# Retention in two rows, sample parts side by side, paced queues: one change to a hybrid encoder step

## The chip, the core and the metric

The kernel runs on one core of one Trainium2 chip. The metric is the device time of one execution in microseconds (us); the time before is 1988.08 us, the median of three runs (1986.14 to 1988.54). The core has TensorE (PE; weight loads are listed as PEld), VectorE (DVE), ScalarE (ACT), GpSimd (POOL) and SyncE (SP), from whose queue all transfers of this kernel are issued. The engines run side by side and wait for each other by semaphores.

## The reference

One layer of a streaming encoder. A prompt of 2048 rows and a sample of 64 rows pass the same weights:

```python
h = rmsnorm(x, norm_g) @ w_in            # 1024 -> 6144 columns
qa, ka, va, za, qb, kb, vb, zb, ga, gb = split(h)
# A: differential attention, 4 heads, two 64-d halves, values 128-d, ALiBi, mask by chunks of 64
p = softmax(qa_c @ ka_c.T / 8 - slope * |i - j|)        # c = 0, 1
oa = (p[0] - lam * p[1]) @ va                            # the sample also sees 4096 cached frames
# B: retention, 4 heads of 128, decay g per head
ob = ((qb @ kb.T) * g**|i-j|) @ vb + (qb * g**(t+1)) @ state
state = g**n * state + kb.T @ (vb * g**(n-1-t))
m = sigmoid(ga) * ((rmsnorm(oa) * silu(za)) @ w_o_diff) + sigmoid(gb) * ((rmsnorm(ob) * silu(zb)) @ w_o_ret)
y = x + m @ w_out
```

Outputs are y for prompt and sample, the normalised keys, the values and the retention states of both.

## The kernel before

Every large product is taken in three matmuls. An operand is split into a rounded high part and the remainder (`xh`/`xl`, `wh`/`wl`), and hi times hi, hi times lo and lo times hi are added up in one PSUM bank.

*Streams.* `w_stream` runs the projections: weights come in pieces (`ws`), ScalarE rounds them (L462), GpSimd takes the remainder (L472), and `mm_group` (L500) multiplies. Columns for values, keys and queries of the attention and values of the retention are computed with tokens on the partitions (`natural`): 128 tokens at a time, and in the first half of the prompt the 64 sample tokens as a last, ninth tile. The others come transposed (`transposed`). A projection's result leaves its `mm` bank through `fin_va`, `fin_qk`, `fin_vb` or `fin_t`, whose copies on ScalarE are L770 and L772 (the latter with a scale), and goes to scratch in DRAM. `z_stream` runs the attention head by head (`qk_block`, scores at L956 and L957, masked on VectorE at L965; `softmax`, exponentials at L995; `at_pv`), after the first half the sample's attention (`sample_attn`, `sample_pv`), and the retention blocks of 128 rows (`ret_block`). When both are through, `out_stream` makes the output: `m_tile` (L1630 to L1632) and `y_tile` (L1698 to L1700), closed by `y_fin` (L1712).

*Order.* The order of PE, ACT and DVE instructions is written by a planner inside the kernel. Each stream is a generator; `loop` takes the first task by priority whose wake time has come. `P`, `A`, `V` and `G` advance a clock per engine by an assumed duration; `take` and `give` hand buffers on with the time at which they come free. PE work of lower priority, mostly projections, so fills the places where a stream has to wait. The order on POOL and SP follows from the order in which instructions are handed out.

*Buffers.* Ten rows of 128 x 1024 (`ROWS`) serve scores, retention and the sample. PSUM has two banks each for `mm`, `s` (scores) and `at` (transposes of the attention, output tiles) and one each for `pv` and `tp`.

*Retention block.* `ret_block` takes two rows (`rqk`, `rvx`) for queries, keys and values, and, when its turn in the chain of states comes, a third (`rru`) for the output. The output is squared (L1434), summed (L1440), normalised (`rsqrt_small`, L229 to L235, then L1446), transposed through `tp` (L1452), copied (L1455) and stored. `ret_some` keeps two blocks alive and returns when the last is done.

*Sample attention.* A head's 64 queries times two halves fill 128 partitions. Its eight units of 512 keys are exponentiated one after the other (L1186). `sample_pv` then sums, moves two sums, the tail and the four halves of the other partitions over by transfers, weighs the two softmax halves (L1274, L1277) and multiplies with the values (L1294). At the end `fold` (L1194) adds the two halves by a matmul.

Of the kernel before, what the change touches and what calls it, by code (L numbers as in the profile page):

```python
# [36 lines left out]
LAT = 250.0  # L37
DMA_LAT = 2600.0
# [22 lines left out]
class Hybrid:  # L61
# [78 lines left out]
    st = ld  # L140
# [26 lines left out]
    def consts(self):  # L167
# [7 lines left out]
        self.fold = c("fold", [128, 64])  # L175
# [47 lines left out]
    def rsqrt_small(self, ms, n, ready):  # L223
# [12 lines left out]
        for _ in range(3):  # L236
            self.tr = self.V(20, self.act)
# [86 lines left out]
    def norm_log(self, j):  # L324
        nc = self.nc
        ss, ms, y, t = self.xin[j][9:]
        nc.scalar.activation(y, ss, AF.Ln, scale=1.0 / D, bias=self.epst[:y.shape[0]])
        nc.scalar.activation(y, y, AF.Exp, scale=-0.5)
        self.A(1, 0, 40)
        self.xin[j].append(self.A(1, 0, 40))  # L330

    def norm_mean(self, j):
        ss, ms, y, t = self.xin[j][9:13]
        self.nc.vector.tensor_scalar(ms, ss, 1.0 / D, EPS, op0=ALU.mult, op1=ALU.add)
        self.V(1, t)

    def norm_root(self, j):
# [6 lines left out]
        for _ in range(3):  # L344
            self.V(20, t2)
# [23 lines left out]
    def x_tile(self, j, wait=True, mid=None):  # L369
# [6 lines left out]
        for q in range(2):  # L376
# [14 lines left out]
            self.give(tag, t2)  # L391
            if q == 0 and mid:
# [98 lines left out]
    def mm_group(self, ps, n, us, wsl, x, wfirst, last, between=None):  # L491
        nc = self.nc
        seg, xsl = x
        for c in range(KC):
# [3 lines left out]
            ops = ((a, xh), (a, xl), (b, xh)) if wfirst else ((xh, a), (xh, b), (xl, a))  # L498
            for i, (p, q) in enumerate(ops):
# [10 lines left out]
    def opening(self, fin):  # L510
# [5 lines left out]
        self.x_alloc(1)  # L516
        us, low = [], []
# [46 lines left out]
        for j in range(1, 9):  # L564
# [15 lines left out]
            ps = self.psum("mm")  # L580
# [3 lines left out]
            self.spawn(fin(ps[:r], r, 1, 128 * j if j < 8 else T, self.pe + LAT), 0, "w")  # L584
            yield self.pe

    def natural(self, half, fin, fresh=False, wide=False):
# [6 lines left out]
        for j0 in range(0, len(tiles), per):  # L594
# [3 lines left out]
            for u, (src, r, seg, col) in enumerate(group):  # L598
                if fresh:
                    yield lambda: len(self.xt_ready) > j0 + u  # L600
                    yield self.xt_ready[j0 + u]
                yield from self.mm_group(ps[:r, n * u:n * u + n], n, us, slice(0, n),
# [4 lines left out]
            self.spawn(fin(ps[:r, :n * len(group)], r, len(group), t0, self.pe + LAT), 0, "w")  # L607
            yield self.pe

# [6 lines left out]
    def fin_qk(self, which, g, nh=2):  # L616
# [4 lines left out]
        def fin(ps, r, nu, t0, t):  # L621
# [16 lines left out]
            self.give("mm", max(t1, t2))  # L638
# [10 lines left out]
            t = self.V(8)  # L649
# [3 lines left out]
            t = self.V(n)  # L653
# [42 lines left out]
    def fin_va(self, g, nh=2):  # L696
# [4 lines left out]
        def fin(ps, r, nu, t0, t):  # L701
# [13 lines left out]
            self.give("mm", max(t2, t3))  # L715
# [17 lines left out]
    def fin_vb(self, g):  # L733
# [3 lines left out]
        def fin(ps, r, nu, t0, t):  # L737
# [5 lines left out]
            self.give("mm", t)  # L743
# [50 lines left out]
    def rms_t(self, ps, n, gain, t, tag, tmp=None):  # L794
# [35 lines left out]
        self.A(n, t)  # L830
# [14 lines left out]
        else:  # L845
            yield t
            nc.vector.scalar_tensor_tensor(out=o, in0=o, scalar=gain, in1=y, op0=ALU.mult, op1=ALU.mult)
            t = self.V(n, t)
# [134 lines left out]
    def softmax(self, st, nk, b, pair):  # L983
# [4 lines left out]
        for units, mx, t in st:  # L988
# [11 lines left out]
        for c in range(2):  # L1000
            lsum = ls[c][:, 0:1]
            if len(rows[0]) > 1:
                lsum = sp.tile([128, 1], F32, tag="a_ls", name="a_ls")
                nc.vector.tensor_add(lsum, ls[c][:, 0:1], ls[c][:, 1:2])
                self.V(1, t)
            nc.vector.reciprocal(w[:, c:c + 1], lsum)
            self.V(1, t)
        nc.vector.tensor_mul(w[:, 1:2], w[:, 1:2], self.nlam)
        t = self.V(1, t)
        yield t  # L1010
        for k, (u0, u1) in enumerate(zip(rows[0], rows[1])):
            n = u0.shape[1]
            nc.scalar.activation(u1, u1, AF.Identity, scale=w[:, 1:2])  # L1013
            t1 = self.A(n, t, 90)
# [3 lines left out]
            t2 = self.V(n, t1)  # L1018
# [73 lines left out]
    def sample_attn(self):  # L1092
# [9 lines left out]
        for h in range(4):  # L1102
# [42 lines left out]
            for m in range(9):  # L1145
# [12 lines left out]
                if m < 8:  # L1158
# [3 lines left out]
                    t = self.V(512, t)  # L1162
# [19 lines left out]
            self.A(64, t, 220)  # L1182
            te = []
            for m in range(8):
                u = units[m // 2][:, (m % 2) * 512:(m % 2) * 512 + 512]
                nc.scalar.activation(u, u, AF.Exp, bias=mx[:, m:m + 1], scale=-1.0, accum_out=lp[:, m:m + 1])  # L1186
                te.append(self.A(512, t, 220))
            self.spawn(self.sample_pv(h, units, both, tail, te, lp, oall), 2, "z")
# [4 lines left out]
        for h in range(4):  # L1193
            nc.tensor.matmul(fp[:, 64 * h:64 * h + 64], oall[:, 128 * h:128 * h + 128], self.fold,  # L1194
# [29 lines left out]
    def v_split(self):  # L1224

        nc = self.nc
        for m in 4 * [*range(9)]:
# [11 lines left out]
            t = self.V(128 * nt, t)  # L1239
# [3 lines left out]
    def sample_pv(self, h, units, both, tail, te, lp, oall):  # L1243
# [7 lines left out]
        l, num, den = (sp.tile([128, 1], F32, tag=k, name=k, bufs=3) for k in ("s_l", "s_num", "s_den"))  # L1251
        nc.vector.tensor_reduce(l, lp[:, :9], axis=AX.X, op=ALU.add)
        nc.vector.tensor_copy(num[lo], l[lo])
        nc.vector.tensor_copy(den[up], l[up])
# [3 lines left out]
        self.ld(num[up], l[lo], 1 << 12)  # L1258
        t = self.ld(den[lo], l[up], 1 << 12)
        tt = sp.tile([64, 64], F32, tag="s_tt", name="s_tt", bufs=2)  # L1260
# [4 lines left out]
        yield t + 600  # L1265
        nc.vector.reciprocal(den, den)
# [665 lines left out]
```

## Time and profile before

| | us |
|---|---|
| median of three runs | 1988.08 |
| profiled execution, its own time | 1990.07 |
| its span | 1988.3 |
| TensorE busy | 1963.8 |
| VectorE busy | 1057.2 |
| ScalarE busy | 991.0 |
| GpSimd busy | 417.3 |

The profile page comes from one execution. A group's row names line, engine, operation, output<-input, shapes and count, then busy time, mean length of one in ns, and the idle time of the engine before it with what ended it. A matmul's printed length runs to the end of its result and overlaps the next one, so the pace is read from start to start. A row of the timeline has the start, the length, engine, line and operation, `rows*columns` of the stationary operand, and in brackets the idle time before it. A row of the list of waits has total, number and longest. `L` numbers are lines of the kernel before; in the changed kernel they are larger.

### The profile page before, as it was taken

Reading aid. Unit: us, or ns where it says so; the run is one execution under the profiler, and the core shown is the slowest. Engines: PE = TensorE matmul, PEld = TensorE weight load, DVE = VectorE, ACT = ScalarE, POOL = GpSimd, SP = SyncE. Lnnn points to the kernel's source line nnn. Section 1 sums busy time; section 2 is a strip of 40 time slices with the busy share of each in tenths; the row PEclk is TensorE's granted clock in tenths of the full one; section 3 lists DMA queues with packets and bytes.
Section 4 is the critical chain, followed back from the end, with each engine's and each line's share of the span. In section 5 each row is a group of like instructions: output and inputs, shape, how many; then the busy total and the mean of one; then the engine's idle time right before and its main releaser. Section 6 shows DMA issues by size and latency. Waiting matters only on the chain.

```text
span 1988.3 us, 34106 instructions
## 1 busy us (share of the span) xinstructions
PE 1963.8 (99%) x12206; PEld 1754.7 (88%) x12206; DVE 1057.2 (53%) x2786; ACT 991.0 (50%) x2185; POOL 417.3 (21%) x383
## 2 busy tenths in 40 slices
PE   9999999999999999999999999999999999999999
PEld 7778989998998989999998888888888888889997
DVE  6453665446565326547756656525644356444432
ACT  6432666655454436436757656635744544333330
POOL 2310121212121221221111111211122434222210
PEclk9999999999999999999999999999999999999999
DMA  7646553335665756664352342652233666444431
GB/s 245 200 143 177 138 157 118 117 87 152 174 174 152 174 151 196 200 187 137 102 153 81 109 137 62 175 146 85 70 98 114 202 219 206 141 130 148 131 93 53
DMA packets 332508, 285.21 MB, mean 143 GB/s; under 512 B 65905, under 2 KB 297329, under 8 KB 332338
## 3 DMA queue, kind: packets, MB, share of 16 engines
q1 hardware_dynamic: 332338, 283.03, 48.5%
q8 instruction: 96, 1.57, 0.3%
q14 instruction: 74, 0.61, 0.1%
HBM read 187.19 MB, written 91.49 MB: 140 GB/s over the span
## 4 chain that ended last, share of the span: by engine, by line
PE 64%; DVE 2%; DMA 2%; ACT 1%; issue 0%; POOL 0%; SPq 0%; POOLq 0%; ACTq 0%; DVEq 0%
PE mm L500 31%; PE at L1698 3%; PE at L1699 3%; PE at L1700 3%; PE s L956 2%; PE s L957 2%; PE at L1063 2%; PE mm L1630 2%; PE s L1632 2%; PE mm L1631 2%; PE mm L1632 2%; PE s L1631 2%; PE s L1630 2%; PE pv L1043 1%; PE pv L1042 1%; PE pv L1041 1%
## 5 line engine op out<-in xcount | busy, mean ns | idle before, releaser
L500 PE MATMUL mm<-xh,wh 128*128 128x512 f32 (+2 forms) x1280 | 459.3, 359 | 2.8 <-ACT ev L770 2.8
L500 PE MATMUL mm<-xh,wl 128*128 128x512 f32 (+2 forms) x1280 | 452.4, 353 | 0.0
L500 PE MATMUL mm<-xl,wh 128*128 128x512 f32 (+2 forms) x1280 | 451.8, 353 | 0.0
L472 POOL TENSOR_TENSOR wl<-ws,wh 128x512 fp32r<-128x512 f32 x189 | 258.6, 1381 | 867.2 <-ACT wh L462 605.5
L500 PE MATMUL mm<-wh,xh 128*128 128x256 f32 (+3 forms) x864 | 273.5, 317 | 0.3 <-DVE tlo L713 0.3
L500 PEld LDWEIGHTS mm<-xh,wh 128*128 128x128 f32 x1280 | 241.4, 189 | 32.4 <-ACT ev L770 3.3
L500 PEld LDWEIGHTS mm<-xh,wl 128*128 128x128 f32 x1280 | 241.1, 188 | 31.9 <-POOL wl L472 0.4
L500 PE MATMUL mm<-wh,xl 128*128 128x256 f32 (+3 forms) x864 | 267.9, 310 | 0.1
L500 PE MATMUL mm<-wl,xh 128*128 128x256 f32 (+3 forms) x864 | 267.6, 310 | 0.0
L500 PEld LDWEIGHTS mm<-xl,wh 128*128 128x128 f32 x1280 | 241.6, 189 | 27.8
L1078 DVE TENSOR_TENSOR atl<-at,ath 128x512 fp32r<-128x512 f32 (+1 forms) x144 | 93.9, 660 | 159.2 <-ACT ath L1076 159.2
L500 PEld LDWEIGHTS mm<-wh,xh 128*128 128x128 f32 (+1 forms) x864 | 162.8, 188 | 11.8 <-PE s L957 0.4
L500 PEld LDWEIGHTS mm<-wl,xh 128*128 128x128 f32 (+1 forms) x864 | 162.9, 189 | 11.0
L500 PEld LDWEIGHTS mm<-wh,xl 128*128 128x128 f32 (+1 forms) x864 | 162.8, 188 | 10.9 <-DVE xl L389 0.6
L770 ACT COPY ev<-mm 128x512 f32<-128x512 f32 x140 | 71.3, 510 | 191.4 <-PE mm L500 166.4
L995 ACT ACTIVATE row<-row,a_mx 128x1024 f32<-128x1024 f32 (+7 forms) x160 | 153.3, 962 | 17.5 <-DVE a_mx L975 16.3
L965 DVE CUSTOM_DVE_ANT_0 row<-s,dfar 128x512 f32<-128x512 f32 (+2 forms) x192 | 118.2, 631 | 57.7 <-PE s L957 57.1
L462 ACT CAST wh<-ws 128x512 fp32r<-128x512 f32 x192 | 115.4, 618 | 33.2 <-PE mm L500 22.0
L1076 ACT CAST ath<-at 128x512 fp32r<-128x512 f32 (+1 forms) x144 | 78.6, 562 | 100.1 <-PE at L1063 95.2
L956 PE MATMUL s<-K,q 128*128 128x512 f32 (+3 forms) x320 | 118.3, 374 | 4.2 <-DVE a_acc L965 4.2
L957 PE MATMUL s<-K,q 128*128 128x512 f32 (+3 forms) x320 | 115.5, 362 | 0.0
L1016 DVE SCALAR_TENSOR_TENSOR row<-row,a_w 128x1024 f32<-128x1024 f32 (+4 forms) x96 | 102.6, 1074 | 21.5 <-ACT row L1013 21.4
(220 smaller groups left out, 3998.0 us busy)
## 6 DMA issues: line engine op xcount, KB each, us to landing
ws<-in_w_in_dram SPq DMA_DIRECT2D x192, 256.0 KB, 3.2
q<-qT SPq DMA_DIRECT2D x128, 128.0 KB, 3.0
V<-vN SPq DMA_DIRECT2D x24, 512.0 KB, 4.8
K<-kT SPq DMA_DIRECT2D x48, 256.0 KB, 4.1
gt<-gaT SPq DMA_DIRECT2D x64, 132.0 KB, 2.1
gt<-gbT SPq DMA_DIRECT2D x64, 132.0 KB, 2.1
xt<-in_x_prompt_dram SPq DMA_DIRECT2D x16, 512.0 KB, 5.9
kn<-in_cache_k_T_dram SPq DMA_DIRECT2D x32, 256.0 KB, 3.7
```

Source lines behind the costliest of these rows:

```text
L462: self.nc.scalar.copy(h, st)
L472: self.nc.gpsimd.tensor_sub(l, st, h.bitcast(F32))
L500: nc.tensor.matmul(ps, p, q, start=c == 0 and i == 0, stop=c == KC - 1 and i == 2)
L956: nc.tensor.matmul(ps, q1s, kk, start=True, stop=False)
L957: nc.tensor.matmul(ps, q2s, kk, start=False, stop=True)
L965: nc.vector.tensor_tensor_reduce(out=units[k0 // 1024][:, k0 % 1024:k0 % 1024 + n], in0=ps, in1=tab, scale=-SLOPES[h], scalar=3.0e38, op0= ...
L995: nc.scalar.activation(u, u, AF.Exp, bias=mx, scale=-1.0, accum_out=lp[:, k:k + 1])
L1016: nc.vector.scalar_tensor_tensor(out=u0, in0=u0, scalar=w[:, 0:1], in1=u1, op0=ALU.mult, op1=ALU.add)
L1078: nc.vector.tensor_sub(al[:, :w], at[:, :w], ah[:, :w].bitcast(F32))
L1630: nc.tensor.matmul(ps, wh[:, csl], oh, start=kt == 0, stop=False)
L1631: nc.tensor.matmul(ps, wh[:, csl], ol, start=False, stop=False)
L1632: nc.tensor.matmul(ps, wl[:, csl], oh, start=False, stop=kt == 3)
```

## The change

Five things are changed.

1. The sample's hi and lo halves are stored side by side as a stationary operand of 128 columns (`xs`, written by GpSimd). A projection slice of the sample takes two matmuls in place of three: xs with the high weights for both halves of a bank, xh with the low weights for the first. `halves` copies the bank, moves its upper 64 partitions down by a transfer, adds them, and hands on to the old `fin`. The sample's output tile is done the same way (`ms`, `y_halves`), and stands ahead of the last prompt tile.
2. A retention block takes two rows: the output goes to the second half of `rvx`, squares and transposed result to the first half of `rqk`. Up to three blocks are alive, and `ret_some` returns before the last is done; the table row is returned by `ret_end`.
3. The sample's sums are folded by a matmul, and its other transfers (`s_move`) start after each pair of exponentials.
4. Long runs of exponentials and of VectorE operations are handed out one at a time, each when its engine's clock is within 700 ns (`PACE`).
5. The planner's durations are changed throughout, 400 ns (`SLACK`) are added ahead of two kinds of transposes, and a store no longer advances the planner's clock of the transfers.

```diff
+SLACK = 400.0
+PACE = 700.0
-    st = ld
+    def st(self, dst, src, nbytes=0):
+        self.nc.sync.dma_start(dst, src)
+        return self.pe + nbytes / 150.0 + DMA_LAT
...
 # rsqrt_small
-            self.tr = self.V(20, self.act)
+            self.tr = self.V(70, self.act)
...
 # x_tile
+            if r == 64:
+                for k, part in enumerate((hi, lo)):
+                    nc.gpsimd.tensor_copy(self.xs[:, 4 * q:4 * q + 4, 64 * k:64 * k + 64], part)
+                    t2 = self.G(256, t2)
...
 # mm_group
+            if ps.shape[0] == 64:
+                pair = [(ps, xh, b), (both, self.xs[:, c, :], a)]
+                for i, (o, p, q) in enumerate(pair if c else pair[::-1]):
+                    nc.tensor.matmul(o, p, q, start=c == 0 and i == 0, stop=c == KC - 1 and i == 1)
+                    self.P(n)
+                ops = ()
...
+    def halves(self, ps, n, t, fin, t0):
+        yield from self.take("ev")
+        up = self.sb(self.ep, [128, 512], "ev", "up")[:, :n]
+        self.nc.scalar.copy(up, ps)
+        t = self.A(n, t)
+        self.give("mm", t)
+        yield t
+        yield from self.take("tlo")
+        dn = self.sb(self.ep, [128, 512], "tlo", "dn")[0:64, :n]
+        t = self.ld(dn, up[64:128], 256 * n)
+        yield t + 2000
+        self.nc.vector.tensor_add(up[0:64], up[0:64], dn)
+        t = self.V(n, t)
+        self.give("tlo", t)
+        yield from fin(up[0:64], 64, 1, t0, t, "ev")
...
 # fin_qk
-            t = self.V(n)
+            t = self.V(n + 100) + SLACK
...
 # softmax
-                t = self.A(u.shape[1], t, 220)
+                t = self.A(u.shape[1], t, 122)
+                yield self.act - PACE
...
 # sample_attn
+            tt = sp.tile([64, 64], F32, tag="s_tt", name="s_tt", bufs=2)
+            self.spawn(self.s_move(tt, tail[64:128], t, moved), 0, "z")
             for m in range(8):
...
-                te.append(self.A(512, t, 220))
+                te.append(self.A(512, t, 114))
+                if m % 2:
+                    lo, up = slice(0, 64), slice(64, 128)
+                    a, b = (lo, up) if m < 4 else (up, lo)
+                    self.spawn(self.s_move(both[m // 2 % 2][a], units[m // 2][b], te[-1], moved), 0, "z")
+                yield self.act - PACE
...
 # sample_pv
-        self.ld(num[up], l[lo], 1 << 12)
-        t = self.ld(den[lo], l[up], 1 << 12)
-        self.ld(tt, tail[up], 1 << 14)
-        for k in range(2):
-            self.ld(both[k][lo], units[k][up], 1 << 18)
-            t = self.ld(both[k][up], units[2 + k][lo], 1 << 18)
+        yield from self.take("s")
+        ps = self.psum("s")
+        nc.tensor.matmul(ps[:, 0:2], self.fold, l, start=True, stop=True)
...
 # ret_block
-        yield from self.take("row")
-        ru = self.row("rru")
...
-        o, sq = ru[:r, 0:512], ru[:r, 512:1024]
+        o, sq = vx[:r, 512:1024], qk[:r, 0:512]
...
-        t = self.V(512, t2)
+        t = self.V(632, t2) + SLACK
...
-        self.give("row", self.pe, 2)
-        self.give("row", t)
+        self.give("row", t, 2)
 
     def ret_some(self, b0, n):
+        yield lambda: self.live["r"] == 0
...
-            yield lambda: self.live["r"] < 2
+            yield lambda: self.live["r"] < 3
             self.spawn(self.ret_block(k, 128 * (b0 + k), 128, b0 + k == 0), 3, "r")
+        self.spawn(self.ret_end(), 3, "z")
+
+    def ret_end(self):
         yield lambda: self.live["r"] == 0
         self.give("row", self.dve + LAT)
...
 # y_tile
+            if sel is None:
+                pair = [(ps[:64], self.ms[:, ct, 0], wl[:, nsl]), (ps, self.ms[:, ct], wh[:, nsl])]
...
+    def y_halves(self, ps, xt, y, r, t):
+        yield from self.take("wst")
+        yt = self.sb(self.z4, [128, 512], "wst", "oyt")
+        yield t
+        nc.vector.tensor_copy(yt[64:128], ps[64:128])
+        nc.vector.tensor_add(xt, ps[0:64], xt)
+        self.give("at", t)
...
+        t2 = self.ld(yt[0:64], yt[64:128], 1 << 17)
+        yield t2
+        nc.vector.tensor_add(yt[0:64], yt[0:64], xt)
...
 # out_stream
             for tt in range(2):
+                if g == 7 and tt:
+                    yield from self.y_tile(7, None, 64, self.i["x_sample"][0], self.o["y_sample"][0])
...
-        yield from self.y_tile(7, None, 64, self.i["x_sample"][0], self.o["y_sample"][0])
```

More of the change, by code (lines that the diff above doesn't have):

```diff
@@ L493, in mm_group @@
         seg, xsl = x
+        if ps.shape[0] == 64:
+            both = self.both
         for c in range(KC):
@@ L742, in fin @@
             t = self.A(n, t)
-            self.give("mm", t)
+            self.give(bank, t)
             yield t
@@ L1193, in sample_attn @@
         for h in range(4):
-            nc.tensor.matmul(fp[:, 64 * h:64 * h + 64], oall[:, 128 * h:128 * h + 128], self.fold,
+            nc.tensor.matmul(fp[:, 64 * h:64 * h + 64], oall[:, 128 * h:128 * h + 128], self.fold[:, :64],
                              start=True, stop=True)
@@ L1250, in sample_pv @@
         yield te[-1]
[L1251 to L1254, printed above, removed]
+        l = sp.tile([128, 2], F32, tag="s_l", name="s_l", bufs=3)
+        num, den = (sp.tile([128, 1], F32, tag=k, name=k, bufs=3) for k in ("s_num", "s_den"))
+        nc.vector.memset(l, 0.0)
+        nc.vector.tensor_reduce(l[lo, 0:1], lp[lo, :9], axis=AX.X, op=ALU.add)
+        nc.vector.tensor_reduce(l[up, 1:2], lp[up, :9], axis=AX.X, op=ALU.add)
         for _ in range(3):
@@ L1355, in ret_block @@
         yield from self.take("row", 2)
-        qk = self.row("rqk")
-        vx = self.row("rvx")
+        qk, vx = (self.row(k) for k in ("rqk", "rvx"))
         def v3(u, k):
@@ L1790, in w_stream @@
         self.z4 = self.es.enter_context(self.tc.tile_pool(name="p3b", bufs=1))
-        self.ms = [self.z4.tile([128, 8, 64], F32R, tag=f"ms{j}", name=f"ms{j}") for j in range(2)]
+        self.ms = self.z4.tile([128, 8, 2, 64], F32R, tag="ms", name="ms")
         self.spawn(self.out_stream(), 8)
```

143 lines of the change are left out of this document (85 added, 58 removed).

## The prediction

> **What bounds the kernel now.** I read the page's busy shares and chain first, then the list of what TensorE waited for, then the timeline at the places that the change touches.
>
> ```profile
> span 1988.3 us, 34106 instructions
> PE 1963.8 (99%) x12206; PEld 1754.7 (88%) x12206; DVE 1057.2 (53%) x2786; ACT 991.0 (50%) x2185; POOL 417.3 (21%) x383
> PE 64%; DVE 2%; DMA 2%; ACT 1%; issue 0%; POOL 0%; SPq 0%; POOLq 0%; ACTq 0%; DVEq 0%
> ```
>
> TensorE is busy for 1963.8 of 1988.3 us; no other engine passes 53%. So the time is the sum of the matmuls plus about 24.5 us in which TensorE does nothing. Anything done on another engine counts only if TensorE waits for it. The waits, longest first:
>
> ```profile
> PE tp L1452 <- DVE rru L1446: 4.4, 3, 1.6
> PE s L956 <- DVE a_acc L965: 4.2, 6, 1.5
> PE mm L500 <- ACT ev L770: 2.8, 2, 2.2
> PE mm L557 <- ACT wh L462: 2.0, 2, 1.3
> PE tp L667 <- ACT wh L462: 1.9, 1, 1.9
> PE at L312 <- DVE epst L1857: 1.1, 1, 1.1
> PE tp L667 <- DVE raw L652: 0.9, 1, 0.9
> PE tp L381 <- DVE xt L351: 0.9, 1, 0.9
> PE s L1375 <- DMA rqk<-kbT: 0.6, 1, 0.6
> ```
>
> These nine rows come to 18.8 us (columns: total, times, longest). Rows L557, L312 and L381, 4.0 us, are the start, which the change leaves alone. The other 14.8 us lie in the middle, and only 0.6 us of them is a transfer. The kernel has therefore two places to gain: fewer matmuls (no limit but their number), and the 14.8 us.
>
> **Part 1: the sample's matmuls, two in place of three.** The 64 sample rows go through five projection groups (three of 512 columns, two of 256) and the last output tile. Each multiplies 8 slices of depth three times; the change joins the hi and lo halves of the sample as 128 stationary columns, so that a slice costs two. What a matmul costs is read from start to start, since its printed length (0.39) overlaps the next. The first group, then a 256-column one, then the final output tile:
>
> ```profile
> 64.08 0.39 PE L500 MATMUL mm<-wh,xl 128*128 128x512 f32 x1
> 64.31 0.40 PE L500 MATMUL mm<-wh,xh 128*64 128x512 f32 x1
> ...
> 69.59 0.39 PE L500 MATMUL mm<-wh,xl 128*64 128x512 f32 x1
> 69.82 0.40 PE L500 MATMUL mm<-wh,xh 128*128 128x512 f32 x1
> ```
> ```profile
> 202.26 0.28 PE L500 MATMUL mm<-wh,xh 128*64 128x256 f32 x1
> ...
> 204.88 0.28 PE L500 MATMUL mm<-wh,xl 128*64 128x256 f32 x1
> ```
> ```profile
> 1973.19 0.45 PE L1698 MATMUL at<-woh,ms 128*64 128x512 f32 x1
> ...
> 1984.05 0.40 PE L1700 MATMUL at<-woh,ms 128*64 128x512 f32 x1
> 1984.48 0.68 DVE L1712 TENSOR_TENSOR oyt<-at,oxt 64x512 f32<-64x512 f32 x1 [4.84 <-PE at L1700]
> ```
>
> From 64.31 to 69.82 are 24 matmuls, 0.230 us each; 8 fewer save 1.84, in three groups 5.5 us. From 202.26 to 204.88 are 23 steps of 0.114; 8 fewer save 0.9, in two groups 1.8. The output tile's 48 take 0.231 each; 16 fewer save 3.7. Together 11.0 us, all on the engine that is the bound. Added: four small matmuls that fold the sample's softmax sums; the nearest row is the fold at the end of the sample's attention.
>
> ```profile
> L1194 PE MATMUL pv<-fold,oall 128*128 128x64 f32 x8 | 1.0, 268 | 0.0
> ```
>
> Four matmuls leave eight records, at most 1.0 us; I take 1.0 (bounds 0.3 and 1.0). Net gain 10.0 us. The four matmuls replace two small transfers per head that nobody on TensorE waited for.
>
> **What joining costs elsewhere.** In the first group the joined operand xs is made by four GpSimd copies of 128x256 after the sample's transposes.
>
> ```profile
> 58.12 3.78 POOL L472 TENSOR_TENSOR wl<-ws,wh 128x512 fp32r<-128x512 f32 x3 [4.99 <-DMA vN<-tlo]
> L840 POOL TENSOR_TENSOR r_y<-r_y,r_sq 128x256 f32<-128x256 f32 x33 | 25.7, 777 | 275.4 <-DVE r_sq L837 207.7 <-PE mm L500 40.3 <-PE s L957 13.8
> ```
>
> GpSimd is free at 61.9, four copies at up to 0.78 us end by 65.0, and the group starts at 64.31, the later slices 1.8 us after that. Its bounds are 0 and 0.7 plus a queue of one split (1.3); I take 0.5. The split weights queued behind the copies are not needed before the next group. After each sample group the two halves are added: a copy on ScalarE, a transfer within SBUF and an add on VectorE. Nobody on TensorE waits for them, as the PSUM bank goes free after the copy, earlier than before; if that cover failed, one bank would be late by the transfer, for which the nearest row is
>
> ```profile
> both<-row SPq DMA_DIRECT2D x16, 256.0 KB, 3.5
> out_y_prompt_dram<-oyt SPq DMA_DIRECT2D x32, 256.0 KB, 2.4
> ```
>
> 3.5 us. At the end the sample's output moves ahead of the last prompt tile. That tile's first matmul reuses the bank that now needs a VectorE copy and an add, 2 x 0.68, against one add before: with the second half's two matmuls in between, about 0.9 us more (0 to 2.0). After the last matmul there is still one add and one store, of 256 KB in place of 128 KB; from the 2.4 us row I put 0.3 on it. Sum of the additions so far 1.7.
>
> **Part 2: queues paced, durations measured.** The order of PE, ACT and DVE is written by a planner; the change raises its durations, adds 400 ns before transposes that follow a normalisation, and lets long runs of instructions be handed out one at a time. No instruction gets cheaper; what changes is how much other PE work stands between a producer and its consumer. One wait shows the mechanism: eight exponentials of one sample head in a row on ScalarE, and the copy that frees a PSUM bank behind them.
>
> ```profile
> 482.26 0.71 ACT L1186 ACTIVATE row<-row,s_mx 128x512 f32<-128x512 f32 x1
> ...
> 489.69 0.35 ACT L770 COPY ev<-mm 128x256 f32<-128x256 f32 x1
> ```
> ```profile
> 490.10 0.50 PE L500 MATMUL mm<-xh,wh 128*128 128x512 f32 x1 [2.24 <-ACT ev L770]
> ```
>
> In the changed order this head's first copies stand between its exponentials, so the 2.2 us should go; I take the row L500 <- L770 from 2.8 to 0.6. The other mechanism is a chain whose cost the planner undercounts: the retention block's normalisation.
>
> ```profile
> 737.78 0.69 DVE L1440 TENSOR_REDUCE ms<-rru 128x4 f32<-128x512 f32 x1 [1.33 <-ACT rru L1434]
> ...
> 741.03 1.19 DVE L233 SCALAR_TENSOR_TENSOR sm_t<-sm_y 128x4 f32<-128x4 f32 x1 [2.36 <-ACT sm_y L230]
> ...
> 744.75 0.69 DVE L1446 TENSOR_TENSOR rru<-rru,sm_y 128x512 f32<-128x512 f32 x1
> ```
>
> From 737.78 to 745.44 (744.75 + 0.69) it took 7.7 us, and three tiny operations in it 1.2 each. In the instruction order of both kernels I counted the matmuls between a block's last retention matmul and its transposes, at 0.45 ns a column for large ones and 0.11 us for 128 columns: the five shortest gaps of the 17 were 4.9, 6.2, 6.3, 6.8 and 7.0 us and become 7.1, 7.8, 8.7, 9.7 and 9.7 (an estimate from paces). So I take row L1452 from 4.4 to 1.0, for two blocks that still fall short of such a chain. The transposes after the q and k norms (L667, 2.8 in two rows) had shortest gaps of 4.3 and now 5.0, median 6.7 and now 8.3: 2.8 to 0.7. Row L956 (4.2) is scores that wait for a bank of two; gaps under 1 us fall from eight to two in that order, which I put at 2.7 left. The sum: 3.4 + 2.1 + 2.2 + 1.5 = 9.2 us (bounds: 0, if the waits only move, and 14.8).
>
> **Part 3: retention blocks of two rows, three at once.** Nothing is computed less. A block keeps its two rows until its stores land, and a third block may start; the next head's scores need no longer wait for the last block. Projection matmuls fill every gap, so freedom of order is worth nothing to TensorE except through the waits. The cost: all blocks share one bank for transposes (tp), and the shortest gap in which it is handed on becomes 1.3 us. I put 0.8 us on it (0 to 2). Where ten rows do not do for the scores as well, a head is late, but covered: the last retention transposes stand some 90 us of matmuls before the last projection in the new order, 70 before.
>
> **Sum.** 10.0 + 9.2 - 1.7 - 0.8 = 16.7 us off. The profiled execution took 1990.07 us, so 1973.4; the median of the three runs (1988.08) lies 1.99 below that execution, so **1971.4 us**.
>
> **Against a rule of the chip's notes.** Whether joined operands come for free hangs on alternating stationary widths: the new loop goes from 64 columns to 128 and back in each of 56 slices. The rows at 64.08 and 69.59 cross such a change and keep the 0.23 us pace. The Trainium skill, "TensorEngine Tiling (Array Packing)", section "Tiling Modes", says that switching the tiling mode drains the engine; by the drain that this case's matmuls show (0.39 printed against 0.23 of pace, so 0.16) the sum would lose 112 x 0.16 = 17.9 us and come to no change. The trace disagrees for columns at these rows.
>
> **The rivals.**
> - *The width switch drains after all* (the other side). A change in the number of rows does cost something:
> ```profile
> 512.52 0.38 PE L1294 MATMUL pv<-vhl,atp 64*128 64x256 f32 x1
> 512.83 0.50 PE L500 MATMUL mm<-xh,wh 128*128 128x512 f32 x1
> ```
> The 64-row matmul takes 0.31 to the next start where 256 columns take 0.114: 0.19 for a switch. At that price 112 switches cost 21.3 us and the kernel ends at 1992.7, slower than before; at the 0.16 between a printed length and the pace it ends at 1989.3, which is no change. The gain is gone at 16.7 / 112 = 0.15 a switch. Against it: columns are not rows, and the rows at 64.08, 64.31 and 69.59 show nothing. 0.04, half of it at each price.
> - *The matmuls alone*: the waits only move. 1971.4 + 9.2 = 1980.6. For it: an order that avoids nine waits can make nine others. 0.22.
> - *All waits of the middle go*: 14.8 in place of 9.2, so 1965.8. For it: the gaps grew at every kind of consumer that I counted. Against: some waits come from tiny VectorE operations of 1.2 us, which a longer gap covers only in part. 0.15.
> - *Three blocks in flight jam the one tp bank*: if each of the 17 blocks (16 and the sample's) waits once for as long as the L1452 row has it on average, 4.4 / 3 = 1.5 us, that is 25 us, of which 1.8 is in the sum already; the kernel ends at 1995. It decides from 16.7 / 17 + 0.1 = 1.1 us a block. For it: all transposes pass one bank. Against: ScalarE, which frees it, is at 50%. 0.05.
>
> **The chances.** The forecast, with a range of its own from 1967 to 1977, holds 0.46. Of the 0.08 that is left, 0.03 is faster by less than the matmuls alone, 0.04 no change (waits that move and additions at their upper bounds, 1990.07 - 10.0 + 7 - 1.99 = 1985 and above), 0.01 slower. So faster 0.46 + 0.22 + 0.15 + 0.03 = 0.86, no change 0.02 + 0.04 = 0.06, slower 0.02 + 0.05 + 0.01 = 0.08. A measurement of this kernel tells about 0.2% (4 us) from no change. The time lies in 1962 to 1983 8 times in 10: at the low end all waits are gone and the additions are next to nothing (1990.07 - 10.0 - 14.8 - 2.0 = 1963.3), at the high end the waits have moved and the additions cost some 2 us more than I put on them.
>
> **What would show it.** Right: 56 fewer big matmuls, 128-column xs rows 0.23 apart from their 64-column neighbours; PE busy about 10 us less; row L1452's successor at 1 us or less; no wait for an ev copy behind a row of exponentials; one wait of about 1 us ahead of the last output tile. Wrong: 0.3 or more between joined matmuls; a new row of several us in TensorE's list, above all for tp, pv, a DMA or a weight split; or a middle in which the old waits return at other places.

## The result, and the profile after

| | before | after |
|---|---|---|
| median of five runs, us | 1988.54 | 1970.64 |
| lowest and highest, us | 1986.14, 1991.79 | 1968.34, 1972.41 |
| ratio, 95% interval | | 0.9907 [0.9895, 0.9919] |
| profiled execution, its own time, us | 1990.07 | 1968.34 |
| its span, us | 1988.3 | 1966.6 |

The change makes the kernel 17.9 us faster, by the medians. The forecast was 1971.4.

The page of the changed kernel, the lines that answer to those of the kernel before:

```profile
span 1966.6 us, 34036 instructions
PE 1951.9 (99%) x12158; PEld 1752.2 (89%) x12158; DVE 1050.3 (53%) x2795; ACT 992.8 (50%) x2190; POOL 418.1 (21%) x387
PE 94%; DVE 3%; DMA 1%; ACT 1%; issue 0%; POOL 0%; SPq 0%; ACTq 0%; POOLq 0%; DVEq 0%
```

TensorE is still the bound. Between the two profiled executions the span falls by 21.7 us: 11.9 us of it is TensorE's busy time (1963.8 to 1951.9), 9.8 us its idle time (24.5 to 14.7). The two profiled executions are not at their medians, one lies 1.5 us above and the other 2.3 below, which is why 21.7 and 17.9 differ.

What TensorE waited for in the changed kernel (total, times, longest), the first eight rows:

```profile
PE s L996 <- DVE a_acc L1005: 1.9, 3, 0.8
PE mm L574 <- ACT wh L470: 1.9, 2, 1.2
PE pv L1349 <- DVE vhl L1286: 1.8, 3, 1.0
PE at L316 <- DVE epst L1938: 1.1, 1, 1.1
PE pv L385 <- DVE xl L393: 0.9, 1, 0.9
PE tp L385 <- DVE xt L355: 0.7, 1, 0.7
PE pv L1349 <- DVE atp L1380: 0.5, 1, 0.5
PE s L997 <- DMA q<-qT: 0.4, 1, 0.4
```

The three rows of the transposes behind norms (4.4, 1.9 and 0.9) and the row of the bank behind exponentials (2.8) are gone. The row of 1.9 is put down to a rounding of weights on ScalarE, but the product that these transposes read (L652) was itself done only at 982.55 us, and they started at 982.70. New are 1.8 and 0.5 us for the sample's values and weights (L1349).

The timeline of a sample group, the widths of the stationary operand taking turns:

```profile
65.03 0.39 PE L512 MATMUL mm<-wl,xh 128*64 128x512 f32 x1
65.26 0.39 PE L512 MATMUL mm<-wh,xs 128*128 128x512 f32 x1
65.49 0.39 PE L512 MATMUL mm<-wl,xh 128*64 128x512 f32 x1
```

They start 0.23 us apart. The Trainium skill's "TensorEngine Tiling (Array Packing)", section "Tiling Modes", says that a change of the tiling mode drains the engine; for these widths the trace shows no drain. A change of rows, from whose cost the forecast priced its first rival, is not in this loop.

Where the idle time went, by stretch. The columns are start and end, length, then busy time of PE (with its matmuls), PEld, DVE, ACT and POOL, granted clock, DMA share, GB/s. The kernel before, then the changed one:

```profile
60.00:430.00 370.00, 367.20 (x2252) 325.24 (x2251) 197.73 (x595) 190.92 (x435) 66.58 (x56) 1.00 0.50 142
430.00:690.00 260.00, 257.18 (x1599) 233.44 (x1598) 137.26 (x319) 129.28 (x300) 52.68 (x38) 1.00 0.59 162
690.00:1000.00 310.00, 303.53 (x2327) 290.96 (x2326) 180.08 (x463) 160.76 (x365) 58.79 (x45) 0.99 0.54 160
```
```profile
60.00:430.00 370.00, 369.36 (x2280) 331.43 (x2279) 198.37 (x606) 197.11 (x449) 68.96 (x60) 1.00 0.51 146
430.00:690.00 260.00, 257.37 (x1590) 232.72 (x1590) 133.30 (x313) 125.63 (x292) 53.40 (x39) 1.00 0.64 173
690.00:1000.00 310.00, 308.76 (x2409) 298.36 (x2407) 183.56 (x483) 165.94 (x376) 54.74 (x43) 1.00 0.52 155
```

In the first stretch (the first heads) TensorE's idle time goes from 2.8 to 0.6 us, in the third (retention, then the second half's projections) from 6.5 to 1.2. In the second, the sample's attention, it stays: 2.8 and 2.6. So the wait of 2.2 us that the forecast showed there went, and others took its place.

Because a matmul's printed length is 0.39 us at a pace of 0.23, stalls below some 0.15 us lie hidden in "busy". I therefore also summed, start to start, what the matmuls took beyond their usual pace (0.231 us for 512 columns, 0.119 for 256, 0.110 for 128 and so on). The net sum of this lost time is 39.1 us before and 28.5 after; in the middle stretch it is 7.3 before and 8.4 after, of which 0.5 are the new matmuls of the fold, which count in full.

### The profile page after: what moved, and what is told of

It reads as the page before. It is cut to its first block, busy times and chain, and to the rows that moved or that the text cites. A ratio compares the mean times of both kernels' runs of the same rounds, so it can differ in the third digit from the quotient of the medians.

```text
span 1966.6 us, 34036 instructions
## 1 busy us (share of the span) xinstructions
PE 1951.9 (99%) x12158; PEld 1752.2 (89%) x12158; DVE 1050.3 (53%) x2795; ACT 992.8 (50%) x2190; POOL 418.1 (21%) x387
## 4 chain that ended last, share of the span: by engine, by line
PE 94%; DVE 3%; DMA 1%; ACT 1%; issue 0%; POOL 0%; SPq 0%; ACTq 0%; POOLq 0%; DVEq 0%
PE mm L516 53%; PE s L996 3%; PE s L997 3%; PE at L1104 3%; PE at L1758 3%; PE at L1759 3%; PE at L1760 3%; PE pv L1084 2%; PE pv L1083 2%; PE pv L1082 2%; PE s L1687 1%; PE mm L1687 1%; PE s L1685 1%; PE mm L1686 1%; PE s L1686 1%; PE mm L1685 1%
## 5 line engine op out<-in xcount | busy, mean ns | idle before, releaser
L516 PE MATMUL mm<-wh,xh 128*128 128x256 f32 (+1 forms) x824 | 258.4, 314 | 0.4 <-ACT raw L672 0.2
L516 PE MATMUL mm<-wh,xl 128*128 128x256 f32 (+1 forms) x824 | 253.4, 307 | 0.0
L516 PE MATMUL mm<-wl,xh 128*128 128x256 f32 (+1 forms) x824 | 253.1, 307 | 0.0
L516 PEld LDWEIGHTS mm<-wh,xh 128*128 128x128 f32 x824 | 156.8, 190 | 9.9 <-ACT raw L672 0.6
L516 PEld LDWEIGHTS mm<-wl,xh 128*128 128x128 f32 x824 | 156.9, 190 | 8.9
L516 PEld LDWEIGHTS mm<-wh,xl 128*128 128x128 f32 x824 | 156.8, 190 | 8.1
```

What stands on the lines that cost most here:

```text
L516: nc.tensor.matmul(ps, p, q, start=c == 0 and i == 0, stop=c == KC - 1 and i == 2)
```

## The experiments

The kernel before, run beside each group of experiments, had medians of 1988.0 to 1989.1. Each experiment was run four to ten times; differences between two experiments under about 2 us are within their spread. The theory was that two gains stand side by side: matmuls that are no longer made, and waits that the planner's new figures avoid, while the retention's new freedom is worth nothing.

### E1: the sample in three matmuls again

```diff
 # the changed kernel, mm_group and y_tile
-            if ps.shape[0] == 64:
-                pair = [(ps, xh, b), (both, self.xs[:, c, :], a)]
...
 # out_stream
-                if g == 7 and tt:
-                    yield from self.y_tile(7, None, 64, ...)
+        yield from self.y_tile(7, None, 64, ...)
```

> The changed kernel with the sample multiplied in three matmuls again, in its old place at the end, everything else as changed. Theory (two separate gains: matmuls and waits): TensorE gets 56 matmuls back, 11.0 us by the paces 0.230 and 0.114, so about 1981 against the changed kernel's 1970.6; TensorE's listed waits stay near the 10 us of the changed kernel. Rival (the sample part also took waits away, since its banks go free earlier and its group is shorter): 1984 or more, with waits of 13 us or more. Rival (joining gives part of its gain back in copies and transfers): 1977 or less.

1982.38 us (0.9966 [0.9953, 0.9978] of the kernel before), 11.7 us above the changed kernel. Its listed waits come to 11.6 us, near the 10 of the changed kernel. This kernel keeps the fold's matmuls, so the forecast for what it undoes is 11.0 us of matmuls less 1.7 of additions, 9.3. That was short: nothing is seen to be given back. Between the profiled executions TensorE's busy time rises by 12.4 us and its idle time by 1.7.

### E2: only the sample's parts side by side

```diff
 # the kernel before, with the joined operand, halves, y_halves and the new place of the output tile
+            if ps.shape[0] == 64:
+                pair = [(ps, xh, b), (both, self.xs[:, c, :], a)]
...
```

> The kernel before with only the sample's parts side by side and its output tile moved ahead of the last one. Theory: 11.0 us of matmuls go and the waits stay near 20 us, so about 1978 against 1988.5. Rival (the gain is eaten by waits that a planner with the old durations makes new when anything moves): above 1983, with waits of 24 us or more. Rival (waits fall as well): below 1974.

1975.23 us (0.9930 [0.9917, 0.9944]), 12.9 us below the kernel before. That lies between the theory's 1978 and the 1974 below which the rival of falling waits stood, and nearer to the latter. Both are seen: TensorE's busy time falls by 10.2 us (1963.8 to 1953.6), and its listed waits fall too, from 19.7 to 16.4 us, where the theory had them stay. The bank behind exponentials is unchanged, and the transposes of the retention still wait, 2.8 us in place of 4.4:

```profile
PE mm L512 <- ACT ev L806: 2.8, 2, 2.2
PE tp L1488 <- DVE rru L1482: 2.8, 2, 1.5
```

So this one part alone brings 12.9 of the 17.9 us, and the planner, the pacing, the retention and the sample's new sums together no more than 4.6 on top of it (1975.23 to 1970.64).

### E3: the old retention

```diff
-        o, sq = vx[:r, 512:1024], qk[:r, 0:512]
+        yield from self.take("row")
+        ru = self.row("rru")
+        o, sq = ru[:r, 0:512], ru[:r, 512:1024]
...
-            yield lambda: self.live["r"] < 3
+            yield lambda: self.live["r"] < 2
...
-        self.spawn(self.ret_end(), 3, "z")
```

> The changed kernel with the old retention: a third row for the output, two blocks alive, the stream waiting for the last block. Theory (freedom of order is worth nothing under a busy TensorE): 1970.6 within 2 us, no new row above 2 us in TensorE's list of waits. Rival (overlap is part of the gain): 1974 or more, with a wait for a row or at the transposes of a block. Rival (three blocks on the one bank for transposes cost something): 1968 or less.

1971.16 us (0.9914 [0.9900, 0.9927]), 0.5 above the changed kernel: no difference. Two rows, three blocks and the overlap with the next head move work about under an engine that always has other work.

### E4: all of the planner's old figures

```diff
-SLACK = 400.0
+SLACK = 0.0
...
-                yield self.act - PACE
...
-            t = self.V(632, t2) + SLACK
+            t = self.V(512, t2) + SLACK
...
```

> The changed kernel with the planner's old durations, no extra 400 ns ahead of transposes, no handing out one at a time, and stores that advance the transfer clock again; sample parts and retention stay as changed. Theory: the same matmuls, and the waits of before come back, 9 us more, so about 1980, with rows for transposes behind the norms and for a bank behind exponentials. Rival (the waits went with the retention's change or the sample's, not with the planner's figures): within 3 us of 1970.6.

1981.38 us (0.9962 [0.9949, 0.9974]), 10.7 above the changed kernel, as expected. But it is also 6 us above E2, whose planner is the old one too. Something in the other parts must cost, under the old figures. The next four separate this.

### E5: without pacing

```diff
                 t = self.A(u.shape[1], t, 122)
-                yield self.act - PACE
...
                     self.spawn(self.s_move(both[m // 2 % 2][a], units[m // 2][b], te[-1], moved), 0, "z")
-                yield self.act - PACE
...
             self.V(1134)
-            yield self.dve - PACE
...
-            yield self.dve - PACE
+            yield self.pe
```

> The changed kernel, but exponentials and the sample's VectorE operations are handed out in one go again. Theory (the run of exponentials ahead of a bank's copy is one of the two mechanisms): 2 to 3 us slower than the changed kernel, 1973, with a wait of about 2 us of a projection for an ev copy. Rival (the new durations alone put the copy in time): within 1.5 us, no such wait.

1983.58 us (0.9974 [0.9965, 0.9984]), 12.9 above the changed kernel, where 2 to 3 were expected. TensorE's list, the two longest rows, and the middle stretch:

```profile
PE mm L516 <- ACT ev L810: 6.3, 4, 2.3
PE mm L516 <- POOL wl L480: 2.9, 3, 1.9
```
```profile
430.00:690.00 260.00, 249.10 (x1518) 221.96 (x1517) 134.08 (x324) 123.89 (x296) 55.30 (x39) 0.99 0.64 171
```

TensorE is idle for 10.9 us in the sample's attention. The mechanism is the one that the forecast showed, a bank's copy behind exponentials on ScalarE; its size was wrong by far: 2 to 3 us were expected because the row had 2.8 in the kernel before, and it has 6.3 here, beside 1.9 in this stretch for a weight remainder of GpSimd. The start-to-start sum for this stretch is 22.2 us against 8.4.

### E6: without the 400 ns

```diff
-SLACK = 400.0
+SLACK = 0.0
```

> The changed kernel without the extra 400 ns ahead of the transposes that follow a normalisation; durations and pacing as changed. Theory (the durations alone lengthen that chain by enough, the 400 ns are a reserve): within 2 us of 1970.6, transposes waiting 1 to 2 us in total. Rival (the chain is late by tiny VectorE operations beside GpSimd, so the reserve does the work): 1974 or more, transposes waiting 4 us.

1978.42 us (0.9952 [0.9938, 0.9965]), 7.8 above the changed kernel: the rival's time, but the transposes wait 2.8 us and not the 4 that it named. The two rows at the head of TensorE's list:

```profile
PE pv L385 <- DVE x_st L338: 3.1, 2, 2.7
PE tp L707 <- DVE raw L692: 2.8, 4, 1.4
```

The second row is the direct effect: the transposes behind the norms are late again, 2.8 us in four places. The first is not, as no 400 ns stands ahead of L385; it came with the order, which moves as a whole when one duration does. The transposes of the retention, the other place of the 400 ns, do not wait here either. So of 7.8 us some 3 are explained by the 400 ns, and the rest came with that order; its waits were not taken apart.

### E7: the old durations

```diff
-    def st(self, dst, src, nbytes=0):
...
+    st = ld
...
-            self.tr = self.V(70, self.act)
+            self.tr = self.V(20, self.act)
...
-            t2 = self.V(n + 110, t1)
+            t2 = self.V(n, t1)
...
```

> The changed kernel with the planner's old durations and the old clock of stores; the 400 ns and the pacing stay. Theory (durations are the larger part of the planner's 10.7 us): 1976 or more. Rival (pacing and the 400 ns do most of it): within 3 us of 1970.6.

1970.44 us (0.9912 [0.9899, 0.9926]): no difference from 1970.64. Some 25 changed figures and the new clock for stores are worth nothing, given the pacing and the 400 ns.

### E8: old figures and old retention

```diff
 # E4 and E3 together
```

> The changed kernel with the planner's old figures as in the fourth experiment, and the old retention as well. It differs from the second experiment's kernel, 1975.2, only in the sample's sums by a matmul and its earlier transfers. Theory (three blocks in flight under wrong durations cost the 6 us by which the fourth experiment, 1981.4, is slower than the second): about 1975. Rival (the sample's early transfers and the folded sums cost them): about 1981, the retention being worth nothing under either set of figures.

1982.89 us (0.9970 [0.9958, 0.9981]): the rival. The retention is worth nothing under the old figures either (1981.38 with the new one). What is left between this kernel and E2's 1975.23 is the sample's sums by a matmul and its early transfers: they cost 7.7 us under the old planner. One row is of the retention itself. With the old one the transposes of the retention wait here, and with the new one, in E4, they do not:

```profile
PE tp L1502 <- DVE rru L1496: 1.9, 2, 1.6
```

The times of E4 and E8 differ by 1.5 us, which is within their spread.

### E9: the sample's old sums, with pacing

```diff
-            self.spawn(self.s_move(tt, tail[64:128], t, moved), 0, "z")
...
-        nc.tensor.matmul(ps[:, 0:2], self.fold, l, start=True, stop=True)
...
+        self.ld(num[up], l[lo], 1 << 12)
+        t = self.ld(den[lo], l[up], 1 << 12)
+        self.ld(tt, tail[up], 1 << 14)
+        for k in range(2):
+            self.ld(both[k][lo], units[k][up], 1 << 18)
+            t = self.ld(both[k][up], units[2 + k][lo], 1 << 18)
+        yield t + 600
```

> The changed kernel with the sample's old sums: two small transfers in place of the matmul, and the transfers of the halves after the last exponential; pacing stays. Theory (the folded sums and early transfers bring nothing by themselves and only need the pacing): within 2 us of 1970.6, the stretch from 430 to 690 us with 6 to 9 us of lost time. Rival (they shorten the sample's chain for TensorE): 1973 or more.

1965.93 us (0.9891 [0.9875, 0.9906]), with runs from 1965.44 to 1967.02: the fastest kernel of the study, 4.7 us below the changed one, whose fastest run was 1968.34. The middle stretch:

```profile
430.00:690.00 260.00, 259.77 (x1605) 236.41 (x1605) 125.16 (x309) 125.22 (x292) 51.03 (x39) 1.00 0.61 170
```

TensorE is idle there for 0.2 us in place of 2.6, and the start-to-start sum is 3.3 us in place of 8.4. The waits of the sample's values (L1349, 1.8 and 0.5) are not in this kernel's list. This part of the change is a loss in each of three pairs of kernels: 4.7 us here, 7.7 under the old planner (E8 against E2) and 5.7 without pacing (E5, 1983.58, against the next).

### E10: the old sums, without pacing

```diff
 # E9 and E5 together
```

> As the ninth, and without handing out one at a time. Theory (the 13 us of the fifth experiment come from the new sums standing behind unpaced exponentials): 1971 to 1975, a bank waiting about 3 us behind exponentials as in the kernel before. Rival (the pacing is needed by the exponentials whatever the sums): 1980 or more.

1977.89 us (0.9949 [0.9936, 0.9961]), 12.0 above E9. The time lies between the bounds of the theory (1975) and of the rival (1980), and the differences speak for the rival: the pacing is worth 12.0 us with the old sums and 12.9 with the new ones. Its longest row is the bank behind exponentials again, 3.6 us, and this stretch is not the only one that loses:

```profile
60.00:430.00 370.00, 368.15 (x2271) 329.72 (x2271) 203.18 (x604) 195.26 (x448) 68.07 (x60) 1.00 0.51 146
430.00:690.00 260.00, 256.00 (x1565) 231.59 (x1565) 139.17 (x316) 125.37 (x294) 57.26 (x40) 0.99 0.63 170
690.00:1000.00 310.00, 305.58 (x2366) 294.62 (x2365) 182.39 (x463) 160.30 (x366) 54.70 (x43) 0.99 0.51 153
```

Idle are 1.9, 4.0 and 4.4 us. By the start-to-start sums, E10 loses 1.9, 6.4 and 4.0 us more than E9 in these three stretches. Yet E2, unpaced and with old figures throughout, has 1975.23. New figures and the 400 ns without pacing bring nothing.

### E11: weight remainders on VectorE

```diff
-        if n in (5, 7, 8):
+        if n not in (1, 2, 3, 4, 6):
             self.nc.vector.tensor_sub(l, st, h.bitcast(F32))
```

> The changed kernel with nearly all weight remainders taken on VectorE in place of GpSimd. Theory (tiny VectorE operations last up to 1.2 us only while a GpSimd operation runs): those of the normalisation fall to 0.17 us beside no GpSimd work; VectorE carries 128 us more and goes to about 59%. For the time two effects oppose; I expect 1969 to 1976. Rival (they are slow for another reason): their lengths stay spread up to 1.2 us.

1978.65 us (0.9954 [0.9942, 0.9967]), 8.0 above the changed kernel and above the range that I gave. VectorE rises to 56%, not 59%, and GpSimd falls from 418 to 171 us. One of the three tiny operations of the retention's normalisation, as a group (busy us, mean ns), in the kernel before, the changed one and this one:

```profile
L234 DVE TENSOR_TENSOR sm_t<-sm_t,ms 128x4 f32<-128x4 f32 x16 | 7.7, 484 | 0.6
```
```profile
L238 DVE TENSOR_TENSOR sm_t<-sm_t,ms 128x4 f32<-128x4 f32 x16 | 3.7, 234 | 0.5
```
```profile
L238 DVE TENSOR_TENSOR sm_t<-sm_t,ms 128x4 f32<-128x4 f32 x16 | 2.6, 163 | 0.6
```

Its mean length falls to 163 ns with GpSimd's remainders gone, so those were what made it long. The time rose by other waits: the first row of the list is transposes of the input behind VectorE, 3.2 us.

### E12: the halves of every output tile one after the other

```diff
-        first = 8 if sel is None else 7
+        first = 8
```

> The changed kernel with the two halves of every output tile finished one after the other, as the sample's tile has it, in place of both together. Theory: each tile's first bank is free before the next tile starts, so the seven or eight waits of about 0.5 us go and one VectorE add of 0.7 us leaves the end: 3 to 5 us less, 1966 to 1968. Rival (the last slice of the merged gates comes too late in this order): at or above 1970.6, with new waits at the first output matmuls.

1968.95 us (0.9907 [0.9893, 0.9920]), 1.7 below the changed kernel and not clear of its spread. What ended the idle time ahead of L1758, in the changed kernel and in this one (us, times):

```profile
  DVE oyt L1791: 3.6, 7
```
```profile
  ACT mh L1714: 2.4, 2
```

The first row is idle time of the weight loads, 0.52 us at each of seven tiles. The matmuls there start 0.48 and then 0.33 us apart in place of twice 0.23, so a tile loses about 0.35 us. The second row is one place, counted once for the weight load (1.4) and once for the matmul (1.0), the eighth slice of the first tile:

```profile
PE at L1758 <- ACT mh L1714: 1.0, 1, 1.0
```

Theory and rival are both seen: the seven waits for a bank go, and one wait for the last slice of the merged gates comes. The add that was to leave the end was not there to be saved (see below).

## Why the prediction was right, and where its steps were not

*The total.* The forecast's 16.7 us are 9.3 for the sample side by side (11.0 of matmuls less 1.7 of additions), 8.4 for the planner and the retention (9.2 less 0.8), and a loss of 1.0 for the fold. The medians allow the same steps. From the kernel before to E2, the first part alone, the time falls by 12.9 us. From E2 to E9, which adds the planner's figures, the 400 ns, the pacing and the retention, it falls by 9.3. From E9 to the changed kernel, which adds the sample's sums, it rises by 4.7. So both gains are there, the waits in about their size, but that the median was hit to 0.8 us is luck: the first part brought 3.6 us more than forecast, and the sample's sums cost 3.7 more.

*The matmuls.* Forecast 11.0 us less 1.0 for the fold. TensorE has 48 records fewer (12206 to 12158), 56 matmuls gone and eight records of the fold added, and is busy for 11.9 us less. The side-by-side part shows 11.7 us (undone, E1) and 12.9 (done alone, E2, with some waits in it), additions included. Right in place and size. The added fold took 1.1 us of printed length in eight records, as taken; from start to start it is 0.14 a matmul, 0.5 in all.

*What joining costs elsewhere.* Forecast 1.7 us of losses; none is seen, so this term was mis-sized. The GpSimd copies were taken at up to 0.78 us each, by a row with two inputs; these have one and took 0.37 each:

```profile
61.53 0.74 POOL L398 CAST xs<-xh 128x256 fp32r<-128x256 f32 x2 [1.11 <-ACT xh L392]
62.22 0.75 POOL L398 CAST xs<-xl 128x256 fp32r<-128x256 f32 x2
```

All four are done at 62.97, before the group starts at 64.12. The 0.9 us ahead of the last prompt tile rested on a misreading of mine: I took the sample's halves to end together, but the line that E12 edits lets them end one after the other and the prompt tiles' together. The first bank was free in time, and the next tile keeps the pace:

```profile
1951.38 0.40 PE L1754 MATMUL at<-woh,ms 128*128 128x512 f32 x1
1951.61 0.39 PE L1758 MATMUL at<-woh,mh 128*128 128x512 f32 x1
...
1962.48 0.40 PE L1760 MATMUL at<-woh,ml 128*128 128x512 f32 x1
```
```profile
1962.22 1.39 DVE L1791 TENSOR_TENSOR oyt<-at,oxt 128x512 f32<-128x512 f32 x2 [6.64 <-PE at L1760]
```

Of these two adds the first begins at 1962.22, while TensorE still works, and the second at 1962.92, after the last matmul (1962.48 + 0.40). So one add stands behind the last matmul, as forecast, and E12 could not take one away. From the start of the last matmul to the end of the span it is 4.1 us, as before (1984.05 to 1988.3, 4.25); the 0.3 for the larger store is not seen.

*The waits.* Forecast 9.2 us less of 14.8. The rows came out as follows: transposes of the retention 4.4 to nothing (forecast 1.0), transposes behind the q and k norms 2.8 to nothing (0.7), the bank behind exponentials 2.8 to nothing (0.6), scores 4.2 to 1.9 (2.7), and 2.3 us new at the sample's values. TensorE's idle time fell by 9.8, of which 3.7 came with E2's kernel, without a new figure. The size was right, its cause only in part. I named durations, the 400 ns and the pacing together. E7 shows the durations to be worth nothing; undoing the 400 ns costs 7.8 (E6), undoing the pacing 12.9 (E5), undoing all three 10.7 (E4). The parts do not add up, so none of them has a price of its own.

The step that failed is the one from longer gaps to the transposes of the retention. The gaps did grow, but the row of 4.4 us is gone also without the 400 ns (E6) and with all of the old figures (E4); of E1 to E10 it stands only where the old figures and the old retention meet (2.8 in E2, 1.9 in E8). The count of matmuls ahead of these transposes, made over by the forecast's paces in the order of the traces, has 4.8, 6.0, 6.2, 6.8 and 6.8 us as the shortest gaps of the kernel before and 4.6, 4.8, 6.0, 6.3 and 6.6 in E4, where no such transpose waits. What ended this row stays open.

*The retention.* Forecast a loss of 0.8; E3 and E8 show no effect on the time that is clear of the spread. The rival of the jammed bank is refuted: TensorE has no wait at L1504.

*The sample's sums.* The forecast priced the fold's matmul at 1.0 us and held that nobody on TensorE waited for what it replaces. The second is true, and the replacement is still a loss of 4.7 us (E9). This is the term of the sum that was mis-sized most. In the changed kernel TensorE waits for the sample's value remainders and weights instead, 2.3 us that E9 does not have; whether the fold or the earlier transfers bring these waits was not separated.

*The rivals.* The width switch did not drain. "The matmuls alone" was put at 1980.6; E2's kernel, which has only them, took 1975.23, and the changed one is faster still. "All waits of the middle go" meant 22.3 us off. The profiled pair fell by 21.7, but not for that reason: 11.9 of it is busy time, and the idle time fell by 9.8, near the 9.2 of the sum and not the 14.8 of the rival. The 5.0 us by which the pair exceeds the sum of 16.7 are 1.9 more of busy time, 0.6 more of idle time and 2.5 of losses that did not come. The medians fell by 3.8 less than the pair, since the two profiled executions stand on either side of theirs.

Not settled is where the pacing gains. Undone with the new sums (E5) it loses time in the sample's attention, 13.8 us by the start-to-start sums; undone with the old sums (E10) it loses 6.4 there and 5.9 in the stretches on either side. No experiment paces one stretch alone. And each edit of a figure moves the whole order, so one kernel per edit cannot tell a wait from the order that came with it, as E6 shows.

## What to carry to other kernels

When one engine is busy for 99%, count its instructions first: joining two half-empty operands was worth 11.7 to 12.9 of 17.9 us here, and no price on the other engines was seen. In an order that is written ahead of time, look first for long runs handed to an engine whose queue also frees the bound engine's banks: handing them out one at a time was worth 12 to 13 us in this kernel, while some 25 corrected durations were worth nothing. Take a change with several parts apart: here one part (the sample's sums) cost 4.7 us under cover of the others.

## What the runs showed of the hardware

A VectorE operation on four columns took 1.2 us where the same takes 0.16. In the kernel before:

```profile
741.03 1.19 DVE L233 SCALAR_TENSOR_TENSOR sm_t<-sm_y 128x4 f32<-128x4 f32 x1 [2.36 <-ACT sm_y L230]
742.26 1.22 DVE L234 TENSOR_TENSOR sm_t<-sm_t,ms 128x4 f32<-128x4 f32 x1
```
```profile
740.90 1.30 POOL L1370 TENSOR_TENSOR rvx<-rqk,rtab 128x512 f32<-128x512 f32 x1
742.15 2.54 POOL L472 TENSOR_TENSOR wl<-ws,wh 128x512 fp32r<-128x512 f32 x2
```

Each ends about when a GpSimd operation ends: 742.22 and 742.20, 743.48 and, of two in a row from 742.15 to 744.69, the first at half. Of all 153 operations of these lines in the kernel before (L233 to L235, four or eight columns), 121 ran beside no GpSimd operation and took 164 ns on average, 32 ran beside one and took 877. In the changed kernel 14 did, with 590; in E11, with the remainders on VectorE, one of 153. The Trainium skill's "GPSIMD Engine Reference", section "Specifications", says that GpSimd shares its SBUF interfaces with VectorE and contends with operations of two SBUF inputs; the traces agree and give the price. How many run beside GpSimd goes with the order: 21 without the 400 ns (E6), but 8 with all of the old figures (E4) and 26 without pacing (E5), and the times of these kernels do not follow the count. Moving the work off GpSimd cured the operations and lost the time elsewhere (E11).

Changing the stationary operand between 64 and 128 columns cost nothing in 56 pairs: apart from two steps of 0.31 and 0.33 us, the matmuls of 512 columns start at most 0.24 us apart and those of 256 at most 0.14. A 64-row matmul of 256 columns took 0.31 us to the next start in the forecast's row, where 256 columns between matmuls of 128 rows take 0.12.
